# The second attention pass reads regrouped queries and keys: a hybrid encoder layer on one core

## The chip, the core and the metric

The kernel runs as one program on one core of a Trainium2 chip. The metric is the device time of one execution in microseconds (us), as the median of the runs taken. In the text PE is TensorE (the matrix engine, PEld its weight loads), DVE is VectorE, ACT is ScalarE, POOL is GpSimd and SP is SyncE, whose queue issues most of the DMAs.

## The reference

One encoder layer on 2048 tokens of width 1024, in float32. After an RMS norm, one projection yields the inputs of two mixers: a bidirectional gated linear attention (GLA, 4 heads) and a dilated attention of 8 heads of width 64. Their outputs go through `w_out`, and a mixture of 32 experts follows. The change is in the dilated attention:

```
DILATED_PATTERNS = ((128, 1), (512, 4), (2048, 16))
for window, dilation in DILATED_PATTERNS:
    # tokens i with the same i mod dilation form a sequence; in it, |i - j| <= 64
    o, lse = banded_attention(to_classes(q), to_classes(k), to_classes(v), 64)
w = softmax(stack(lses)); o = sum over patterns of w * o
```

Pattern 0 takes the tokens as they stand. Pattern 1 takes every 4th token (4 classes of 512), pattern 2 every 16th (16 classes of 128).

## The kernel before, in words

The program goes through the projections (in which a first attention pass finds each row's maximum and sum), then a stage that holds the second attention pass and the whole GLA, then `w_out` with the router, then the experts. The change is in the second of these stages, about 759 to 1197 us of the profiled execution.

Queries and keys of a head lie in SBUF with their 64 features in the partitions and the 2048 tokens along the row. They are kept as a high and a low part, so `aq` and `ak` (high) and `bq` and `bk` (low parts, with two extra rows that subtract the joint log-sum) give one score block by two matmuls that accumulate. `att_load` brings them for one head, into `pb0` or `pb1` by the head's parity.

The pass has 8 heads of 24 steps, 8 for each pattern (`att_steps`). A step takes two blocks. `att_scores` first adds the band's mask by a matmul with an identity (line 619, or line 622 twice, for blocks whose masks differ), then runs the two matmuls of each block (lines 625 and 626): the block's 128 keys are the stationary operand, 256 queries stream. ACT writes the exponentials to a buffer `pt` (lines 630 and 632). `att_values` multiplies them with the values (line 660), four steps later (`ATT_LAG`); there are five `pt` buffers (`PPB`). For patterns 1 and 2 the operands are strided views: every 4th or every 16th token of the row, for keys and for queries. A step of pattern 1 takes one block each of two classes that are two apart (4 blocks a class); in pattern 2 a step's mask has half the width, and two steps share one call of `att_values`.

Beside it run GLA's pieces (`all_gla`), emitted at 0.9 of a piece per attention step: a state scan on DVE (lines 785 and 788), the decays (lines 363 to 388), the preparation (lines 750 to 763) and the output (lines 802 to 858), for each of 4 GLA heads in turn, so that one GLA head takes two attention heads. Its gates are loaded into `sg` (line 826), of which there are two buffers.

Each engine runs its instructions in order. The order is made at build time by a planner that simulates the engines; only the expert stage's order is written by hand. Buffers of a pool are given out by the same planner: the value tiles and the raw rows of `w_out` share three buffers `vt`.

Of the kernel before, what the change touches and what calls it, by code (L numbers as in the profile page):

```python
# [25 lines left out]
P = 128  # L26
# [16 lines left out]
GLA_WAIT = 6  # L43
ATT_LAG = 4
LEAD = 3
# [12 lines left out]
NRAW, NSPL, CRAW = 8, 4, 6  # L58
PPB = 5
PSS, PSO, PSG = 4, 1, 2  # L60
# [30 lines left out]
def tile_trunk(ctx, tc, x, norm1_w, w_in, gfw, gfb, gbw, gbb, gnw, w_out, norm2_w, rgw, rgb, rew, reb,  # L91
# [77 lines left out]
    def block(p, b):  # L169

        if p == 2:
            return (lambda t: t[:, b::16]), (lambda t: duo(t, b)), am[:, 768:896], 0
        st, c, j, nj = (1, 0, b, 16) if p == 0 else (4, *divmod(b, 4), 4)
        k0 = min(max(P * j - 64, 0), P * nj - 256)
        v = (P * j - k0) // 64
        return (lambda t: t[:, c::st][:, P * j:P * j + P]), (lambda t: t[:, c::st][:, k0:k0 + 256]), \
            am[:, 256 * v:256 * v + 256], k0 * st // 16

    def joint_lse(half, pS, tiles):
# [366 lines left out]
    pb = [cw_.enter_context(tc.tile_pool(name=n, bufs=1, reuse_waits="tile")) for n in ("pb0", "pb1")]  # L546
    WO = []
    with ExitStack() as cb:
        vp = cb.enter_context(tc.tile_pool(name="vp", bufs=3, reuse_waits="tile"))
        pp = cb.enter_context(tc.tile_pool(name="pp", bufs=PPB, reuse_waits="tile"))  # L550
# [5 lines left out]

        BB = [[pb[e].tile([P, S], F32R, name=n) for n in ("bq", "bk")] for e in range(2)]
        for bq, bk in BB:
            for t, one in ((bq, 0.0), (bk, 1.0)):
                G.memset(f32(t)[0:64], 0.0)  # L560
                V.memset(f32(t)[0:2], one)

        def att_load(h):

            aq, ak = [pb[h % 2].tile([P, S], F32R, name=n) for n in ("aq", "ak")]
            bq, bk = BB[h % 2]
            load_twice(SY, f32(ak), khS[h])
            for t, src in ((aq, qS[h, 0:128]), (bk[64:128], klS[h]), (bq[64:128], qS[h, 64:128]), (bq[0:2], qS[h, 128:130])):
                SY.dma_start(f32(t), src)
            return aq, ak, bq, bk  # L570

# [12 lines left out]
        def wout_load(k):  # L584

            raw = vp.tile([P, D], F32, name="vt")
            SY.dma_start(raw, w_out[0, k * P:(k + 1) * P, :])
            t = pb[k // 4].tile([P, 2, D], F32R, name=("aq", "ak", "bq", "bk")[k % 4])
            A.copy(t[:, 0], raw)
            (G if k < 4 else V).tensor_tensor(t[:, 1], raw, f32(t[:, 0]), op=ALU.subtract)  # L590
            WO.append(t)

# [4 lines left out]
        def att_steps():  # L597

            for h in range(8):
                for b in range(8):  # L600
                    yield h, 0, (b, b + 8)
                for b in range(8):
                    yield h, 1, (b, b + 8)
                for c in (0, 4, 1, 5, 2, 6, 3, 7):
                    yield h, 2, (c, c + 8)

        def att_scores(h, p, blocks):
            if h not in ATT:
                ATT[h] = att_load(h)
            aq, ak, bq, bk = ATT[h]  # L610
            ps = psS.tile([P, 512], F32, name="psS")
# [5 lines left out]

            if p or blocks[0] not in (0, 7):
                ATT["last"] = T.matmul(sv[:, :, o:o + n], identb, mask(0, 2), start=True, stop=False, skip_group_check=True)
# [3 lines left out]
            for e, b in enumerate(blocks):  # L623
                ks, qs, _, _ = block(p, b)
                T.matmul(sv[:, e], ks(ak), qs(aq), start=False, stop=False, skip_group_check=True)  # L625
                T.matmul(sv[:, e], ks(bk), qs(bq), start=False, stop=True, skip_group_check=True)  # L626
            if p < 2:
# [7 lines left out]
        def att_values(h, p, blocks, pts):  # L635
# [21 lines left out]
            if p == 2:  # L657
                val = [(b // 8, b, (m, b % 8), pts[e // 2][:, 256 * (e % 2) + 64 * m:256 * (e % 2) + 64 * m + 64]) for m in range(2) for e, b in enumerate(blocks)]
            for hf, b, d, src in val:
# [12 lines left out]
        def attention():  # L672
            steps = list(att_steps())
            pend = []
            LAG = ATT_LAG
            for t in range(len(steps) + LAG):
                if t < len(steps):
                    h, p, blocks = steps[t]
# [12 lines left out]
                if t >= LAG:  # L691
                    h, p, blocks, pt = pend.pop(0)
                    if p < 2:
                        att_values(h, p, blocks, [pt])
                    elif t % 2 == LAG % 2:
                        ATT["even"] = blocks, pt
                    else:
                        b1, p1 = ATT.pop("even")
                        att_values(h, p, b1 + blocks, [p1, pt])
                    if (t - LAG) % 24 == 23:  # L700
# [92 lines left out]
        def gla_out(g):  # L793
# [30 lines left out]
            def gate_load(i4):  # L824
                sg = gs.tile([P, 4, P], F32, name="sg")
                SY.dma_start(sg, ggS[512 * i4:512 * i4 + 512, cols].rearrange("(i p) n -> p i n", p=P))
                return sg
# [49 lines left out]
        def all_gla():  # L877
# [6 lines left out]
            for g in range(4):  # L884
                yield from gla_scan(g)
                if g < 3:
# [5 lines left out]
        work2 = all_gla()  # L892
        lz = gp.tile([P, 192], F32, name="lz")
        work3 = joint_lse(1, psS, lambda n: gs.tile([P, 4, P], F32, name=(None, "oe", "sg", "sg")[n]).rearrange("p i n -> p (i n)")
                          if n else lz)
        cred = 0.0
# [799 lines left out]
```

## Time and profile before

| | us |
|---|---|
| median of 3 runs (2322.39 to 2325.31) | 2322.49 |
| the profiled execution | 2324.34 |
| its span from the first to the last instruction | 2322.6 |
| PE busy | 2112.9 (91%) |
| DVE busy | 1409.6 (61%) |
| ACT busy | 1281.8 (55%) |
| POOL busy | 1014.8 (44%) |

Busy time is a sum over stages that have different limits; an engine's share of the whole span says little about one stage. A matmul's record covers its latency, and successive matmuls overlap, so the cost of one to PE is the distance from its start to the next one's start.

### The profile page before, as it was taken

The page shows a single profiled execution, that of the slowest core. Times are in us where ns is not written, and L with a number is a line of the kernel's source. Part 1 is how long each engine was busy: PE and PEld are TensorE (multiplying, and loading weights), DVE is VectorE, ACT ScalarE, POOL GpSimd, SP SyncE. Part 2 cuts the span into 40 slices and gives each one's busy share as a digit, 9 for nine tenths or more (in the row PEclk, how much of TensorE's full clock was granted, in tenths as well). Part 3 has the DMA queues.
Part 4 walks back from the last instruction along what each step waited for, and adds up shares of the span by engine and source line. Part 5 has one row for each costly group of instructions (what it writes and reads, how often), then busy time and mean ns, then how long its engine had stood idle before and what let it go on. Part 6 is the DMA issues. An engine that isn't in the chain of part 4 may idle for free.

```text
span 2322.6 us, 38346 instructions
## 1 busy us (share of the span) xinstructions
PE 2112.9 (91%) x13813; PEld 1710.3 (74%) x13813; DVE 1409.6 (61%) x2871; ACT 1281.8 (55%) x2286; POOL 1014.8 (44%) x602
## 2 busy tenths in 40 slices
PE   7999998989799799999979999588898999999975
PEld 6888897989799677878768887366665666666654
DVE  7865544545365373626434666479876777768676
ACT  5222666657486464747442333356665767676744
POOL 4766111020120111202020001388887998888866
PEclk9999999999999899999989999799999999999988
DMA  8745765575642969685454643688988999999973
GB/s 308 233 107 151 183 181 163 149 207 147 175 124 69 217 152 187 145 193 113 114 149 151 212 155 127 214 269 282 328 272 279 327 326 329 300 317 295 310 279 151
DMA packets 283475, 487.09 MB, mean 210 GB/s; under 512 B 77079, under 2 KB 155927, under 8 KB 276096
## 3 DMA queue, kind: packets, MB, share of 16 engines
q1 hardware_dynamic: 238512, 368.40, 51.1%
q0 software_dynamic: 29344, 110.03, 17.0%
q10 hardware_dynamic: 15424, 6.16, 1.1%
q8 instruction: 110, 1.80, 0.3%
q14 instruction: 85, 0.70, 0.1%
HBM read 392.01 MB, written 94.44 MB: 209 GB/s over the span
## 4 chain that ended last, share of the span: by engine, by line
PE 71%; DVE 13%; DMA 9%; issue 3%; ACT 2%; POOL 1%; SPq 1%; ACTq 0%; another core or an unknown queue 0%; DVEq 0%; POOLq 0%
DMA wraw<-in_w_in_dram 5%; PE pg L1315 4%; PE pg L1317 4%; PE pg L1316 4%; DVE wlo L991 4%; PE psm L161 3%; PE po L1302 3%; PE psm L150 3%; PE psm L152 3%; PE psm L162 3%; PE psm L151 3%; PE psm L160 3%; PE po L1076 3%; PE po L1074 3%; PE po L1078 3%
## 5 line engine op out<-in xcount | busy, mean ns | idle before, releaser
L991 POOL TENSOR_TENSOR wlo<-raw,whi 128x2048 fp32r<-128x2048 f32 x97 | 513.3, 5302 | 87.0 <-ACT whi L986 83.0
L991 DVE TENSOR_TENSOR wlo<-raw,whi 128x2048 fp32r<-128x2048 f32 x95 | 372.6, 3931 | 64.0 <-ACT whi L986 64.0
L986 ACT CAST whi<-raw 128x2048 fp32r<-128x2048 f32 x192 | 366.8, 1910 | 53.2 <-PE pg L1383 36.6
L161 PE MATMUL psm<-wl,uhi 128*128 128x256 f32 (+1 forms) x768 | 222.9, 291 | 1.1 <-DVE wl L142 1.1
L160 PE MATMUL psm<-wh,uhi 128*128 128x256 f32 (+1 forms) x768 | 222.7, 290 | 0.7 <-ACT wh L141 0.5
L162 PE MATMUL psm<-wh,ulo 128*128 128x256 f32 (+1 forms) x768 | 221.6, 289 | 0.0
L1315 PE MATMUL pg<-whi,xh 128*128 128x512 f32 x512 | 215.7, 421 | 0.7 <-ACT xh L141 0.7
L495 ACT ACTIVATE je<-st,nm 128x256 bf16<-128x256 f32 (+1 forms) x384 | 178.6, 466 | 52.3 <-DVE nm L492 50.3
L1317 PE MATMUL pg<-wlo,xh 128*128 128x512 f32 x512 | 204.7, 400 | 0.0
L1316 PE MATMUL pg<-whi,xl 128*128 128x512 f32 x512 | 204.3, 399 | 0.0
L630 ACT ACTIVATE pt<-psS 128x512 f32<-128x512 f32 x128 | 131.0, 1074 | 85.3 <-PE psS L626 46.1
L625 PE MATMUL psS<-aq,ak 128*128 128x256 f32 x384 | 172.2, 455 | 0.0
L142 DVE TENSOR_TENSOR wl<-wraw,wh 128x512 fp32r<-128x512 f32 (+1 forms) x140 | 100.6, 738 | 92.5 <-ACT wh L141 92.1
L150 PE MATMUL psm<-uhi,wh 128*128 128x512 f32 (+1 forms) x400 | 153.8, 388 | 0.3 <-ACT wh L141 0.3
L151 PE MATMUL psm<-ulo,wh 128*128 128x512 f32 (+1 forms) x400 | 153.5, 385 | 0.5 <-DVE ulo L142 0.5
L152 PE MATMUL psm<-uhi,wl 128*128 128x512 f32 (+1 forms) x400 | 152.6, 385 | 0.0
L160 PEld LDWEIGHTS psm<-wh,uhi 128*128 128x128 f32 x768 | 150.5, 196 | 1.6 <-ACT wh L141 1.0
L161 PEld LDWEIGHTS psm<-wl,uhi 128*128 128x128 f32 x768 | 150.3, 196 | 1.6 <-DVE wl L142 1.3
L162 PEld LDWEIGHTS psm<-wh,ulo 128*128 128x128 f32 x768 | 149.1, 194 | 0.0
L492 DVE CUSTOM_DVE_ANT_0 st<-psS,am 128x256 f32<-128x256 f32 x256 | 98.6, 421 | 82.9 <-PE psS L483 57.5
L626 PE MATMUL psS<-bq,bk 128*128 128x256 f32 x384 | 141.5, 374 | 0.0
L141 ACT CAST wh<-wraw 128x512 fp32r<-128x512 f32 (+1 forms) x144 | 85.1, 623 | 97.3 <-DMA wraw<-in_w_in_dram 85.6
(420 smaller groups left out, 5097.1 us busy)
## 6 DMA issues: line engine op xcount, KB each, us to landing
raw<-in_expert_w_gate_dram SPq DMA_DIRECT2D x128, 512.0 KB
raw<-in_expert_w_up_dram SPq DMA_DIRECT2D x128, 512.0 KB
raw<-in_expert_w_down_dram SPq DMA_DIRECT2D x64, 1024.0 KB
wraw<-in_w_in_dram SPq DMA_DIRECT2D x128, 256.0 KB
xt<-in_x_dram SPq DMA_DIRECT2D x32, 512.0 KB
aq<-s_q POOLq DMA_DIRECT2D x8, 1024.0 KB, 8.3
kk<-s_khi POOLq DMA_DIRECT2D x16, 512.0 KB, 13.4
ak<-s_khi SPq DMA_DIRECT2D x16, 512.0 KB
```

The source lines that it names most:

```text
L150: T.matmul(ps[:m, ts], wh[:, k, m0:m0 + m], uh[:, k, ts], start=(k == 0), stop=False)
L151: T.matmul(ps[:m, ts], wh[:, k, m0:m0 + m], ul[:, k, ts], start=False, stop=False)
L152: T.matmul(ps[:m, ts], wl[:, k, m0:m0 + m], uh[:, k, ts], start=False, stop=(k == KD - 1))
L160: T.matmul(ps[:, :n], uh[:, k, sl], wh[:, k, :n], start=(k == 0), stop=False)
L161: T.matmul(ps[:, :n], uh[:, k, sl], wl[:, k, :n], start=False, stop=False)
L162: T.matmul(ps[:, :n], ul[:, k, sl], wh[:, k, :n], start=False, stop=(k == KD - 1))
L495: A.activation(je[:, :n], st[:, :n], AF.Exp, bias=nm[:, col:col + 1], scale=-1.0, accum_out=zt[:, col:col + 1])
L986: (A.copy if high is A else high.tensor_copy)(hi, raw)
L991: low.tensor_tensor(lo, raw, f32(hi), op=ALU.subtract)
L1315: T.matmul(pgt[n], xh[:, k], hi[:, 2 * n + kk], start=(k == 0), stop=False)
L1316: T.matmul(pgt[n], xl[:, k], hi[:, 2 * n + kk], start=False, stop=False)
L1317: T.matmul(pgt[n], xh[:, k], lo[:, 2 * n + kk], start=False, stop=(k == KD - 1))
```

## The change

Keys and queries of patterns 1 and 2 are first copied into contiguous tiles.

- Queries: `aq` and `bq` become one tile `qq` (both parts side by side). `in_order`, called at every second step from the 7th on, has POOL copy one group of 512 queries with both parts into a tile `grp` (two buffers): a whole class of pattern 1 in one instruction of 1024 elements a partition, or four classes of pattern 2 in two instructions of 512.
- Keys: `keys_in_order`, called one step ahead, has DVE copy the step's two key blocks, by one instruction of 256 elements for the high and one for the low part, into a tile `kgr` (two buffers).
- The steps' order: a step of pattern 1 takes two blocks of one class, and those at a class's ends need two masks. Pattern 2 goes through the classes in order, and each step has its own call of `att_values`.
- The values lag three steps, with four `pt` buffers; `vt` has two buffers and `sg` one.

```diff
-ATT_LAG = 4
+ATT_LAG = 3
-PPB = 5
+PPB = 4
+    def near(p, b):
+        j, nj = (b, 16) if p == 0 else (b % 4, 4)
+        k0 = min(max(P * j - 64, 0), P * nj - 256)
+        return slice(k0, k0 + 256)
-        vp = cb.enter_context(tc.tile_pool(name="vp", bufs=3, reuse_waits="tile"))
+        vp = cb.enter_context(tc.tile_pool(name="vp", bufs=2, reuse_waits="tile"))
+        def in_order(h, p, g):
+            qq = ATT[h][2]
+            ATT["grp", h, p, g] = t = vp.tile([P, 2, 512], F32R, name="grp", bufs=2)
+            if p == 1:
+                G.tensor_copy(t, qq.rearrange("p e (m c) -> p e c m", c=4)[:, :, g])
+            else:
+                for x in range(2):
+                    G.tensor_copy(t[:, :, 256 * x:256 * x + 256].rearrange("p e (y l) -> p e y l", y=2),
+                                  qq.rearrange("p e (l c) -> p e c l", c=16)[:, :, 8 * x + 2 * g:8 * x + 2 * g + 2])
+        def keys_in_order(h, p, blocks):
+            t = vp.tile([P, 2, 2, P], F32R, name="kgr", bufs=2)
+            for w in range(2):
+                src = ATT[h][w]
+                if p == 1:
+                    c, j = divmod(blocks[0], 4)
...
+                else:
+                    src = src.rearrange("p (l c) -> p c l", c=16)[:, blocks[0]::8]
+                V.tensor_copy(t[:, w], src)
+            ATT["keys", h, p, blocks] = t
-                for b in range(8):
-                    yield h, 1, (b, b + 8)
-                for c in (0, 4, 1, 5, 2, 6, 3, 7):
+                for c in range(4):
+                    yield h, 1, (4 * c + 1, 4 * c + 2)
+                    yield h, 1, (4 * c, 4 * c + 3)
+                for c in range(8):
                     yield h, 2, (c, c + 8)
-            if p or blocks[0] not in (0, 7):
+            if blocks[0] % 4 if p == 1 else p or blocks[0] not in (0, 7):
-                ks, qs, _, _ = block(p, b)
-                T.matmul(sv[:, e], ks(ak), qs(aq), start=False, stop=False, skip_group_check=True)
-                T.matmul(sv[:, e], ks(bk), qs(bq), start=False, stop=True, skip_group_check=True)
+                x = slice(256 * (b // 8), 256 * (b // 8) + 256) if p == 2 else near(p, b)
+                for w, kt in enumerate((ak, bk)):
+                    T.matmul(sv[:, e], kg[:, w, e] if p else kt[:, P * b:P * b + P], qq[:, w, x], start=False, stop=(w == 1), skip_group_check=True)
+                n = t % 24 - 6
+                if t < len(steps) and 0 <= n < 16 and n % 2 == 0:
+                    in_order(steps[t][0], 1 + n // 8, n // 2 % 4)
+                if t + 1 < len(steps) and steps[t + 1][1]:
+                    keys_in_order(*steps[t + 1])
-                    if p < 2:
-                        att_values(h, p, blocks, [pt])
-                    elif t % 2 == LAG % 2:
-                        ATT["even"] = blocks, pt
-                    else:
-                        b1, p1 = ATT.pop("even")
-                        att_values(h, p, b1 + blocks, [p1, pt])
+                    att_values(h, p, blocks, [pt])
-                sg = gs.tile([P, 4, P], F32, name="sg")
+                sg = gs.tile([P, 4, P], F32, name="sg", bufs=1)
```

The high parts of `w_out` that were loaded into `aq` and `bq` at the stage's end now go to the two halves of `qq`, and the small tiles of the joint log-sum share the `oe` and `sg` buffers.

## Rows read from the trace of the kernel before

**Rows 1.** Windows: the stage and its tail; busy us per engine, PE clock, DMA share, GB/s

```profile
759.00:1197.00 438.00, 407.19 (x4383) 339.19 (x4381) 208.19 (x459) 250.71 (x427) 69.85 (x63) 0.95 0.70 155
1197.00:1217.00 20.00, 4.21 (x58) 2.99 (x56) 6.55 (x20) 5.94 (x7) 0.43 (x2) 0.61 0.78 225
```

**Rows 2.** Timeline of PE: a step of pattern 0 (start, length, line, operands)

```profile
1101.10 0.39 PE L619 MATMUL psS<-am,identb 128*128 128x512 bf16 x1
...
1101.56 0.28 PE L625 MATMUL psS<-aq,ak 128*128 128x256 f32 x1
1101.68 0.28 PE L626 MATMUL psS<-bq,bk 128*128 128x256 f32 x1
1101.88 0.66 PE L660 MATMUL pso<-pt,vt 128*64 128x128 f32 x8
1102.47 0.39 PE L622 MATMUL psS<-am,identb 128*128 128x256 bf16 x2
...
1103.27 0.66 PE L660 MATMUL pso<-pt,vt 128*64 128x128 f32 x8
```

**Rows 3.** Timeline of PE: a step of pattern 1

```profile
1103.86 0.39 PE L619 MATMUL psS<-am,identb 128*128 128x512 bf16 x1
...
1104.52 0.44 PE L625 MATMUL psS<-aq,ak 128*128 128x256 f32 x1
1104.76 0.43 PE L626 MATMUL psS<-bq,bk 128*128 128x256 f32 x1
1105.12 0.66 PE L660 MATMUL pso<-pt,vt 128*64 128x128 f32 x8
```

**Rows 4.** Timeline of PE: a step of pattern 2

```profile
857.85 0.28 PE L619 MATMUL psS<-am,identb 128*128 128x256 bf16 x1
...
859.02 0.65 PE L660 MATMUL pso<-pt,vt 128*64 128x128 f32 x6
```

**Rows 5.** Windows: patterns 1 and 2 of heads 0 to 7, in order

```profile
770.50:818.80 48.30, 36.53 (x313) 29.93 (x311) 17.25 (x31) 15.81 (x22) 5.72 (x4) 0.86 1.04 199
835.30:876.70 41.40, 40.93 (x476) 33.60 (x475) 28.12 (x44) 31.93 (x57) 12.00 (x11) 1.00 0.56 122
888.20:926.30 38.10, 33.54 (x304) 28.07 (x303) 9.61 (x27) 14.98 (x22) 1.01 (x1) 0.91 0.83 158
943.80:983.20 39.40, 38.38 (x441) 31.98 (x441) 25.74 (x37) 31.54 (x63) 12.83 (x12) 1.00 0.49 115
1001.20:1035.30 34.10, 33.13 (x297) 27.22 (x295) 6.92 (x17) 13.65 (x21) 0.00 (x0) 1.00 0.76 154
1051.00:1092.10 41.10, 40.69 (x477) 33.37 (x475) 27.59 (x45) 30.09 (x53) 8.46 (x8) 1.00 0.35 73
1103.90:1141.80 37.90, 34.51 (x295) 28.36 (x294) 5.44 (x13) 16.81 (x29) 1.01 (x1) 0.91 0.55 126
1157.10:1200.00 42.90, 41.91 (x544) 35.85 (x544) 17.77 (x44) 23.90 (x58) 11.60 (x10) 1.00 0.37 106
```

**Rows 6.** One line's instructions: a strided DVE copy and a DVE instruction of one element

```profile
L203 DVE COPY sg<-oe x2: 260/263/266, 813.3 to 813.5; 64x128 f32<-64x128 f32 x2
...
L260 DVE TENSOR_SCALAR ss<-ss x16: 133/144/154, 7.0 to 134.5; 128x1 f32<-128x1 f32 x16
```

**Rows 7.** Groups of POOL by line and shape: count, busy us, mean ns

```profile
L590 POOL TENSOR_TENSOR aq<-vt,aq 128x1024 fp32r<-128x1024 f32 x1 | 2.4, 2382 | 46.6 <-ACT aq L589 46.6
...
L711 POOL TENSOR_SCALAR_AFFINE_SELECT tri<-tri 64x64 int8<-64x64 int8 x2 | 0.5, 236 | 2.2 <-DVE tri L708 2.2
masks.py:199 POOL TENSOR_SCALAR_AFFINE_SELECT ident<-ident 128x128 f32<-128x128 f32 x1 | 0.3, 294 | 0.1
```

**Rows 8.** Timeline of DVE around 2231 us, in the expert stage

```profile
2230.88 5.01 DVE L1557 TENSOR_SCALAR xl<-xg,tokl 128x1024 fp32r<-128x1024 f32 x1 [0.82 <-PE pg L1316]
2235.81 0.74 DVE L1557 TENSOR_SCALAR xh<-xg,tokl 128x1024 fp32r<-128x1024 f32 x1
```

**Rows 9.** Timeline of POOL at the same time

```profile
2230.76 4.59 POOL L991 TENSOR_TENSOR wlo<-raw,whi 128x2048 fp32r<-128x2048 f32 x1 [4.96 <-ACT whi L986]
```

More of the change, by code (lines that the diff above doesn't have):

```diff
@@ L546, in tile_trunk @@
     pb = [cw_.enter_context(tc.tile_pool(name=n, bufs=1, reuse_waits="tile")) for n in ("pb0", "pb1")]
-    WO = []
+    WO, WQ = [], {}
     with ExitStack() as cb:
-        vp = cb.enter_context(tc.tile_pool(name="vp", bufs=3, reuse_waits="tile"))
+        vp = cb.enter_context(tc.tile_pool(name="vp", bufs=2, reuse_waits="tile"))
         pp = cb.enter_context(tc.tile_pool(name="pp", bufs=PPB, reuse_waits="tile"))
@@ L555, in tile_trunk @@
         psG = cb.enter_context(tc.tile_pool(name="psG", bufs=PSG, space=PSUM, reuse_waits="tile"))
[L557 to L561, printed above, removed]
+        QQ = [pb[e].tile([P, 2, S], F32R, name="qq") for e in range(2)]
+        BK = [pb[e].tile([P, S], F32R, name="bk") for e in range(2)]
@@ L563, in att_load @@
+        for qq, bk in zip(QQ, BK):
+            G.memset(f32(qq)[0:64, 1], 0.0)
+            G.memset(f32(bk)[0:64], 0.0)
+            V.memset(f32(bk)[0:2], 1.0)
         def att_load(h):
-            aq, ak = [pb[h % 2].tile([P, S], F32R, name=n) for n in ("aq", "ak")]
-            bq, bk = BB[h % 2]
+            ak = pb[h % 2].tile([P, S], F32R, name="ak")
+            qq, bk = QQ[h % 2], BK[h % 2]
             load_twice(SY, f32(ak), khS[h])
-            for t, src in ((aq, qS[h, 0:128]), (bk[64:128], klS[h]), (bq[64:128], qS[h, 64:128]), (bq[0:2], qS[h, 128:130])):
+            for t, src in ((qq[:, 0], qS[h, 0:128]), (bk[64:128], klS[h]), (qq[64:128, 1], qS[h, 64:128]), (qq[0:2, 1], qS[h, 128:130])):
@@ L569, in att_load @@
                 SY.dma_start(f32(t), src)
-            return aq, ak, bq, bk
+            return ak, bk, qq
+        def in_order(h, p, g):
[7 more added lines that the diff above has]
+                                  qq.rearrange("p e (l c) -> p e c l", c=16)[:, :, 8 * x + 2 * g:8 * x + 2 * g + 2])
@@ new lines, in keys_in_order @@
+        def keys_in_order(h, p, blocks):
[4 more added lines that the diff above has]
+                    c, j = divmod(blocks[0], 4)
+                    src = src[:, c::4].rearrange("p (j m) -> p j m", j=4)[:, 0:4:3] if j == 0 else src[:, c::4].rearrange("p (j m) -> p j m", j=4)[:, 1:3]
+                else:
+                    src = src.rearrange("p (l c) -> p c l", c=16)[:, blocks[0]::8]
+                V.tensor_copy(t[:, w], src)
+            ATT["keys", h, p, blocks] = t
@@ L587, in wout_load @@
             SY.dma_start(raw, w_out[0, k * P:(k + 1) * P, :])
-            t = pb[k // 4].tile([P, 2, D], F32R, name=("aq", "ak", "bq", "bk")[k % 4])
+            if k % 4 < 2:
+                WQ[k] = pb[k // 4].tile([P, 2, S], F32R, name="qq") if k % 4 == 0 else WQ[k - 1]
+                t = WQ[k][:, k % 4].rearrange("p (a n) -> p a n", a=2)
+            else:
+                t = pb[k // 4].tile([P, 2, D], F32R, name=("ak", "bk")[k % 2])
             A.copy(t[:, 0], raw)
@@ L609, in att_scores @@
                 ATT[h] = att_load(h)
-            aq, ak, bq, bk = ATT[h]
+            ak, bk, qq = ATT[h]
+            if p:
+                qq = ATT["grp", h, p, blocks[0] // 4 if p == 1 else blocks[0] // 2]
+                kg = ATT.pop(("keys", h, p, blocks))
             ps = psS.tile([P, 512], F32, name="psS")
@@ L657, in att_values @@
             if p == 2:
-                val = [(b // 8, b, (m, b % 8), pts[e // 2][:, 256 * (e % 2) + 64 * m:256 * (e % 2) + 64 * m + 64]) for m in range(2) for e, b in enumerate(blocks)]
+                val = [(b // 8, b, (m, b % 8), pts[0][:, 256 * e + 64 * m:256 * e + 64 * m + 64]) for m in range(2) for e, b in enumerate(blocks)]
             for hf, b, d, src in val:
@@ L892, in tile_trunk @@
         work2 = all_gla()
-        lz = gp.tile([P, 192], F32, name="lz")
-        work3 = joint_lse(1, psS, lambda n: gs.tile([P, 4, P], F32, name=(None, "oe", "sg", "sg")[n]).rearrange("p i n -> p (i n)")
-                          if n else lz)
+        work3 = joint_lse(1, psS, lambda n: gs.tile([P, 4, P], F32, name=("oe", "oe", "sg", "oe")[n], bufs=1 if n == 2 else 2).rearrange("p i n -> p (i n)"))
         cred = 0.0
```

## The prediction

> **What bounds the kernel now.** I read the windows first, then the timeline of PE inside them. In the stage of the second attention pass PE is busy for 407 of 438 us, DVE for 208, ACT for 251 and POOL for 70 [rows 1]: PE is the limit and the other engines look half idle. The timeline shows what PE's time buys. A step of pattern 0 takes 0.78 us from its mask to the next work (1101.10 to 1101.88), and its score matmuls start 0.12 us apart [rows 2]. A step of pattern 1 takes 1.26 us (1103.86 to 1105.12), with starts 0.24 us apart [rows 3], and one of pattern 2 takes 1.17 us (857.85 to 859.02), though its mask is half as wide [rows 4]. The matmuls have the same size in all three; what differs is that the operands are strided. The reader is to see that PE is busy at half speed in two thirds of the steps. Last come the windows by head: where patterns 1 and 2 run, DVE has two faces, 26 to 28 of some 40 us in heads 1, 3 and 5 (GLA's decays and output run there), but 5 to 17 of 34 to 48 in the even heads [rows 5].
>
> **Gain on PE.** With contiguous operands a middle step of pattern 1 should cost what pattern 0's does: 1.26 - 0.78 = 0.48 us saved, 32 steps, 15.4 us. A step at a class's ends now pays two half masks; pattern 0 has such steps too, at 0.80 us (1102.47 to 1103.27) [rows 2], so 0.46 x 32 = 14.7 us. In pattern 2 the mask is 0.28 us long instead of 0.39 [rows 2, 4], so a step should cost 0.78 - 0.11 = 0.67: 0.50 x 64 = 32.0 us. Sum 62 us, 7.75 a head. The value matmuls stay the same in number and size. That all of it is on the path holds as long as nothing else becomes late; ACT's 251 us [rows 1] fit into what is left.
>
> **Key copies on DVE.** Two per step in 128 steps, 256 in all, 32 a head, of 256 elements with a strided source. The nearest row is a strided copy of 128 elements: 0.263 us; an instruction of one element takes 0.144 [rows 6]. So an element costs (0.263 - 0.144) / 128 = 0.93 ns, and a copy 0.144 + 0.238 = 0.38 us. Bounds: 0.26 if the length is nearly free, 0.53 if everything scales. I take 0.38: 12.2 us a head, 97 in all. On average there is room (208 + 97 = 305 of some 400 us). By stretch there isn't. Heads 1, 3 and 5 need 28.1 + 12.2 = 40.3 of 41.4 us, 37.9 of 39.4 and 39.8 of 41.1 [rows 5], so even with DVE never idle they can shrink by only 1.1, 1.5 and 1.3 us instead of 7.75 each: 19 us of the 62 are gone, and 43 are left. Head 7 needs 30.0 of 42.9 and the even heads at most 29.5 of 48.3; these keep theirs.
>
> **Query copies on POOL.** Eight groups a head, 64 in all, each of 1024 elements a partition. No row shows a copy on POOL. Below, two one-input instructions of 64 and 128 elements took 0.236 and 0.294 us, 0.9 ns an element, so 1.1 us a group; above, a two-input one of 1024 elements took 2.38 us [rows 7]. A copy has one input, so I take 1.35 us, nearer the lower end, with something for the stride and for pattern 2's second instruction. That is 86 us in all; POOL itself has the room (70 of 438 busy). The price is elsewhere: DVE's 1024-element instruction on one tensor took 5.01 us where its twin took 0.74, and it ended at 2235.89, just after POOL's instruction that had begun 0.12 us before it and ended at 2235.35 [rows 8, 9]. DVE instructions of this kind stand still while POOL has an operand in hand, and a key copy is of this kind. Where DVE is the limit (heads 1, 3 and 5: 24 groups) I count half a group's 1.35 us, since GLA's instructions that read PSUM fill the rest: 24 x 0.67 = 16 us. In the other heads two steps take 2 x (1.85 - 0.49) = 2.7 us (1.85 from mask 1103.86 to the next step's by the same pattern: 1.26 for scores [rows 3] and 0.59 for the values, as from 1101.88 to 1102.47 [rows 2]), and a group with four key copies wants 1.35 + 1.52 = 2.9: covered to 0.2 us, counted as nothing. If that cover is gone, rival 2 has the price.
>
> [...]
>
> **Given back.** GLA's work on DVE that the copies push aside in heads 1, 3 and 5 can slide into the even heads, where DVE is idle for most of the time [rows 5]. The planner decides; I count a quarter of the 19 + 16 us, 9. Ends: nothing, and all of it.
>
> **Edits at nothing or little.** One buffer less with a lag one shorter leaves the same spare `pt` buffer: nothing, where ACT keeps up as now. One `sg` buffer makes SP hold the next gate load, and every load queued behind it, until the last gate is used; the gate is due a pass later, and only where the DMA share is near 1 (heads 0, 2 and 4 [rows 5]) is it late: 2 us. Two `vt` buffers delay the last `w_out` rows, but PE is busy for 4.2 of the 20 us after the stage [rows 1]: nothing, up to 5 if they come more than that late. In head 0 PE is idle for 11.8 of 48.3 us with the DMAs saturated (share 1.04) [rows 5]; a key copy that the planner put behind a GLA instruction waiting for its load makes that longer: 3 us, between 0 and 8. In general DVE's queue is now on PE's path, since the two `kgr` buffers allow one step's lead.
>
> **Sum.** 62 - 19 - 16 + 9 - 5 = 31 us. The profiled execution took 2324.34 us (1.7 more than its span), 1.85 above the median; 2324.3 - 31 = 2293.3, on the median's scale 2291.5, so 2292.
>
> **Rivals.**
> 1. PE's gain comes nearly whole: the planner spreads GLA, so that DVE's full stretches level out, and POOL's copies are near 1.1 us. For it: 305 us of DVE in some 390. Against it: heads 1, 3 and 5 as they stand. 62 less some 7: 2267.
> 2. Slower: the copies take turns. A group holds DVE's key copies for 1.5 us or more of a time near 2.4 us, with keys only one step ahead. Then patterns 1 and 2 need DVE's time plus 8 x 1.5 = 12 us a head: heads 1, 3 and 5 take 52.3, 49.9 and 51.8 us, 32 more than now; head 7 takes 42.0, 0.9 less; heads 0, 2, 4 and 6 take 41.5, 33.8, 31.1 and the PE floor of 30.2, which saves 6.8, 4.3, 3.0 and 7.7. Sum 32 - 23 = +9, and 5 to 9 for the small terms and a clock that falls in the gaps (0.86 and 0.91 in the stretches where PE waits now [rows 5]): 2322.5 + 16 = 2338. It decides from about 1.3 us blocked a group. For it: rows 8 and 9; against it: POOL's one-input rows. [...]
> 3. The lock and DVE's queue eat just what PE gains: 1.2 us a group gives -6 by the same sum, with 5 of small terms 2321.
>
> That contiguous operands don't run faster is no rival: pattern 0 on the same lines shows it.
>
> **Chances and range.** Forecast (10 to 45 us gained) 0.55; rival 1 0.12; rival 2 0.20; rival 3 0.13. A measurement tells 0.2%, 4.6 us, from no change. Of rival 3 0.08 stay within that, 0.05 are faster: faster 0.55 + 0.12 + 0.05 = 0.72, same 0.08, slower 0.20. The range reaches to most of rival 1 and half of rival 2: 2267 to 2337. The forecast's own is 2278 to 2312.
>
> **What would show it.** Starts of lines 625 and 626 should be 0.12 us apart in all patterns; if they stay at 0.24, the first term falls. Key copies should last 0.38 us alone and up to a group longer where a POOL copy stands beside them; if none is longer, the lock is no matter, and rival 1 gains. PE should wait for `kgr` in heads 1, 3 and 5 above all, hardly in the even ones. POOL copies over 2 us, with PE waiting for DVE in every pair of steps, would make me wrong on the far side.

## Result and profile after

The changed kernel took 2393.13 us (median of 4 runs, 2383.95 to 2404.39) against 2322.59 of the kernel before on the same chip (4 runs): 1.0299 times as long, 95% interval 1.0266 to 1.0332. Forecast were 2292 us and a range of 2267 to 2337. The profiled execution of after took 2404.39 us, 80.1 more than that of before, and it is the slowest of the four; ratios come from all runs, places and durations from this one execution.

Where its 80.1 us lie (first and last score matmul, and first matmul of `w_out`, bound the stretches):

| stretch | before | after | change |
|---|---|---|---|
| start to first score | 759.0 | 779.1 | +20.1 |
| stage, first to last score | 437.8 | 482.4 | +44.6 |
| handover, last score to first `w_out` matmul | 20.3 | 32.0 | +11.7 |
| the rest of the span | 1105.5 | 1109.2 | +3.7 |

Of the first line some 12 us are there at the last projection matmul, and most of them arise between 233 and 268 us, in code that the change doesn't touch and with the DMAs full (share 1.18 from 230 to 250 us, 1.15 in before). The kernel without copies was profiled twice: at 268 us it stood 2.2 us behind the kernel before in one execution and 7.7 in the other. So up to some 8 us of the 20 are variation from run to run. In the rest PE waits for `identb` on DVE just before the first score, 13.9 us against 5.7 before.

The windows of after, the stage and the handover (columns as in [rows 1], which they answer):

```profile
779.10:1261.50 482.40, 410.93 (x4447) 318.45 (x4445) 374.91 (x708) 247.84 (x424) 209.14 (x155) 0.91 0.59 133
1261.50:1293.50 32.00, 3.20 (x27) 2.08 (x26) 7.91 (x24) 8.61 (x11) 5.69 (x5) 0.55 0.70 202
```

DVE is busy for 375 us instead of 208, where 305 were expected; POOL for 209 instead of 70. PE's time outside its busy 411 us rises from 31 to 71, its busy time doesn't fall (407 before), and its mean granted clock falls from 0.95 to 0.91. The part of the change that concerns PE works, though. Its timeline shows a middle and an end step of pattern 1 (start, length, line, operands), against [rows 2, 3]:

```profile
858.03 0.39 PE L658 MATMUL psS<-am,identb 128*128 128x512 bf16 x1
858.07 0.82 PE L665 MATMUL psS<-grp,kgr 128*128 128x256 f32 x4
858.82 0.66 PE L699 MATMUL pso<-pt,vt 128*64 128x128 f32 x8
859.41 0.39 PE L661 MATMUL psS<-am,identb 128*128 128x256 bf16 x2
859.56 0.72 PE L665 MATMUL psS<-grp,kgr 128*128 128x256 f32 x4
860.21 0.33 PE L699 MATMUL pso<-pt,vt 128*64 128x128 f32 x2
```

From mask to values it takes 0.79 us (858.03 to 858.82) where it took 1.26. What went wrong is in the copies. The groups of DVE and of POOL in the stage (count, busy us, mean ns, idle time before them and its end):

```profile
L600 DVE CAST kgr<-bk 128x256 fp32r<-128x256 f32 x126 | 89.3, 709 | 0.1
L600 DVE CAST kgr<-ak 128x256 fp32r<-128x256 f32 x126 | 79.3, 630 | 34.3 <-PE psS L665 33.4
...
L388 DVE TENSOR_TENSOR_SCAN tab<-rm,tab 64x512 f32<-64x512 bf16 x24 | 38.6, 1608 | 6.9 <-POOL tab L385 6.7
```

```profile
L587 POOL CAST grp<-qq 128x512 fp32r<-128x512 f32 x64 | 73.9, 1184 | 62.7 <-PE psS L665 62.7
L584 POOL CAST grp<-qq 128x1024 fp32r<-128x1024 f32 x30 | 67.5, 2251 | 118.0 <-PE psS L665 105.3 <-issue 12.6
```

A key copy takes 0.63 or 0.71 us in the mean. Its median is 0.38 (the one line's instructions: shortest, median, longest ns, and who waited for them):

```profile
L600 DVE CAST kgr<-ak x128: 360/391/2286, 764.4 to 1259.0; 128x256 fp32r<-128x256 f32 x128
L600 DVE CAST kgr<-bk x128: 358/383/5937, 766.2 to 1259.3; 128x256 fp32r<-128x256 f32 x128
...
  PE psS L665: 27.1, 17
  PEld psS L665: 17.6, 12
```

The mean is made by copies that stand beside one of POOL's. One such moment, in DVE's timeline and in POOL's:

```profile
925.50 0.38 DVE L600 CAST kgr<-ak 128x256 fp32r<-128x256 f32 x1
925.80 2.22 DVE L600 CAST kgr<-bk 128x256 fp32r<-128x256 f32 x1
927.93 0.37 DVE L600 CAST kgr<-ak 128x256 fp32r<-128x256 f32 x1
```

```profile
925.68 2.09 POOL L584 CAST grp<-qq 128x1024 fp32r<-128x1024 f32 x1 [3.79 <-PE psS L665]
```

POOL begins at 925.68 and ends at 927.77; the key copy that begins 0.12 us later ends at 928.02, and the next one is short again. It is what [rows 8, 9] showed for another pair of instructions. Nor is it one moment only: of all 256 key copies 64 took over 0.7 us, each of them beside an instruction of POOL (59 beside a query copy); of the 115 that overlap none of POOL's, none took over 0.41 us.

### The profile page after: what moved, and what is told of

The parts are those of the page before. It is cut to its first block, busy times and chain, and to the rows that moved or that the text cites. A ratio compares the mean times of both kernels' runs of the same rounds, so it can differ in the third digit from the quotient of the medians.

```text
span 2402.7 us, 38970 instructions
## 1 busy us (share of the span) xinstructions
PE 2118.0 (88%) x13845; PEld 1690.2 (70%) x13845; DVE 1593.7 (66%) x3125; ACT 1280.4 (53%) x2286; POOL 1161.7 (48%) x698
## 4 chain that ended last, share of the span: by engine, by line
PE 65%; DVE 17%; DMA 9%; issue 4%; ACT 3%; POOL 1%; SPq 0%; ACTq 0%; DVEq 0%; another core or an unknown queue 0%; POOLq 0%
DMA wraw<-in_w_in_dram 5%; PE pg L1352 4%; PE pg L1353 4%; PE pg L1354 4%; DVE wlo L1028 4%; PE psm L161 3%; PE psm L162 3%; PE psm L160 3%; PE psm L150 3%; PE psm L151 3%; PE psm L152 3%; PE po L1339 3%; DVE kgr L600 3%; PE po L1111 3%; PE po L1113 3%
## 5 line engine op out<-in xcount | busy, mean ns | idle before, releaser
L1028 DVE TENSOR_TENSOR wlo<-raw,whi 128x2048 fp32r<-128x2048 f32 x95 | 385.5, 4066 | 64.6 <-ACT whi L1023 64.6
L699 PE MATMUL pso<-pt,vt 128*64 128x128 f32 (+3 forms) x1856 | 143.9, 267 | 12.5 <-ACT pt L669 7.3
L665 PE MATMUL psS<-grp,kgr 128*128 128x256 f32 x512 | 113.7, 335 | 27.4 <-DVE kgr L600 27.1
```

The source lines that it names most:

```text
L1028: low.tensor_tensor(lo, raw, f32(hi), op=ALU.subtract)
```

## The experiments

The runs come from several chips, on which the kernel before took 2322 to 2327 us. So kernels are compared by their ratio to the kernel before on the same chip, and a difference of ratios is given in us of 2323; the medians only stand beside them. Theory 1: POOL's copies hold DVE, and PE waits for DVE. Theory 2: the keys are copied only one step ahead. Theory 3: the side edits cost the time. The table has the 18 runs; "waits" is the stage less PE's busy time in it, the engines' columns are busy us in the stage. Places and durations come from one profiled execution of each kernel.

| kernel | median us | ratio, 95% interval | stage | waits | DVE | ACT | POOL | handover |
|---|---|---|---|---|---|---|---|---|
| before | 2322.59 | 1 | 437.8 | 30.8 | 208 | 251 | 70 | 20.3 |
| after | 2393.13 | 1.0266-1.0332 | 482.4 | 71.5 | 375 | 248 | 209 | 32.0 |
| e1 no copies | 2317.02 | 0.9948-1.0002 | 438.8 | 25.7 | 208 | 251 | 62 | 9.9 |
| e16 the same again | 2321.86 | 0.9964-1.0009 | 435.9 | 24.1 | 207 | 251 | 62 | 10.1 |
| e2 queries, POOL | 2373.00 | 1.0177-1.0230 | 463.4 | 39.1 | 227 | 252 | 200 | 32.5 |
| e3 keys, DVE | 2369.60 | 1.0147-1.0217 | 461.4 | 24.2 | 298 | 252 | 66 | 31.2 |
| e4 queries ACT, keys DVE | 2347.66 | 1.0062-1.0143 | 441.5 | 46.2 | 290 | 356 | 66 | 33.7 |
| e5 queries, ACT | 2353.62 | 1.0063-1.0160 | 441.6 | 31.3 | 206 | 357 | 59 | 33.5 |
| e6 short POOL copies | 2410.61 | 1.0346-1.0432 | 507.0 | 76.5 | 326 | 245 | 303 | 31.2 |
| e7 as e4, keys 3 ahead | 2347.65 | 1.0052-1.0121 | 443.6 | 62.4 | 284 | 357 | 67 | 32.6 |
| e8 as after, keys 3 ahead | 2393.06 | 1.0261-1.0347 | 478.5 | 88.2 | 359 | 246 | 212 | 35.4 |
| e9 queries ACT and DVE | 2333.60 | 1.0017-1.0066 | 424.9 | 59.2 | 323 | 303 | 69 | 33.8 |
| e10 as e9, four row buffers | 2332.71 | 1.0010-1.0067 | 422.9 | 57.6 | 323 | 303 | 69 | 30.1 |
| e11 as e10, even heads | 2347.14 | 1.0050-1.0112 | 441.7 | 44.4 | 262 | 276 | 64 | 28.7 |
| e12 as after, even heads | 2362.83 | 1.0102-1.0202 | 449.2 | 43.4 | 277 | 249 | 133 | 33.5 |
| e13 as e10, rows earlier | 2327.00 | 0.9997-1.0040 | 424.1 | 55.8 | 323 | 302 | 69 | 28.9 |
| e14 as e13, half copies | 2337.13 | 1.0031-1.0078 | 432.9 | 61.6 | 329 | 307 | 70 | 29.5 |
| e15 as e14, GLA rate 1.0 | 2344.41 | 1.0060-1.0117 | 445.0 | 70.6 | 328 | 310 | 70 | 27.2 |
| e17 as e9, keys 1 ahead, own pool | 2340.46 | 1.0050-1.0100 | 443.5 | 40.7 | 327 | 300 | 72 | 17.0 |
| e18 as after, own pool | 2378.08 | 1.0192-1.0258 | 483.6 | 68.0 | 378 | 247 | 212 | 14.3 |

**No copies, one copy, and ACT in POOL's place.** e1 drops both calls and reads the old strided views, e2 keeps the query copies, e3 the key copies, e4 moves the query copies:

```
e1, e2 -  if t + 1 < len(steps) and steps[t + 1][1]: keys_in_order(*steps[t + 1])
e1, e3 -  if t < len(steps) and 0 <= n < 16 and n % 2 == 0: in_order(...)
e4     -  G.tensor_copy(t, qq.rearrange(...)[:, :, g])     # and pattern 2's
       +  A.copy(t, qq.rearrange(...)[:, :, g])
```

> The changed kernel without its query copies on GpSimd and its key copies on DVE: the scores read the strided operands as before, and every other edit stays (order of the steps, values lag 3, four pt, two vt, one sg buffer, the query tile of two rows). Theory 1 (GpSimd's copies hold back DVE's key copies and the other DVE instructions, and PE waits for these): the loss is gone with the copies, 2325 to 2345 us, with score starts 0.24 us apart again; what is above 2322.5 is the price of the side edits. Theory 2 (DVE's queue is too full and only one step ahead, GpSimd or not): the same here. Theory 3 (the side edits cost the time, above all at the stage's two ends): 2375 us or more, since PE also loses its 62 us again.

> The kernel without any copies once more, for its interval: the side edits alone (one order of the steps, lag 3, other buffers). From the first time, 0.9975 of the kernel before; expected 0.994 to 1.000, 2312 to 2325 us. If the 10 us come from the handover (9.9 us from the last score to the first w_out matmul against 20.3), they show again.

2317 and, repeated, 2322 us (0.998 and 0.999 of before): with every side edit in place nothing is lost, so theory 3 falls as it was stated, and e1 lies under the range of theory 1, which had a price for these edits. It is not shown to be faster either. The 10 us of handover did show again.

> The changed kernel with the query copies on GpSimd alone; the keys are read strided, and DVE copies nothing. Theory 1: GpSimd's copies still hold back DVE, but only GLA's instructions, on which PE does not wait step by step. If the moving operand's stride is what doubles the matmul, PE keeps most of its 62 us: 2280 to 2315 us, score starts 0.12 us apart, no PE wait for DVE in pairs of steps. If the stationary operand's stride is what costs, starts stay at 0.24 us and the time is 2325 to 2350. Theory 2: as theory 1, DVE has no key copies here. Theory 3: 2360 or more.

> The changed kernel with the key copies on DVE alone; the queries are read strided, and GpSimd copies nothing. Theory 1: without GpSimd's copies a key copy lasts 0.38 us throughout (mean under 0.45 against 0.63 and 0.71 us), and PE does not wait for them for more than some 5 us in all; the time is that of no copies within 10 us if the moving operand sets the matmul's length, 30 to 50 us less if the stationary one does. Theory 2 (DVE's queue alone is the trouble): PE waits for the key tile in heads 1, 3 and 5 as it does with both copies (over 20 us), and the time is 2365 us or more.

e2 lies above both ranges of theory 1. e3 lies in the branch of theory 2: 2370 us, with 20 us of waits for the keys. Four score matmuls of an end step in e2's PE timeline, with the next line's start:

```profile
916.63 0.47 PE L664 MATMUL psS<-grp,ak 128*128 128x256 f32 x1
916.93 0.40 PE L664 MATMUL psS<-grp,bk 128*128 128x256 f32 x1
917.17 0.40 PE L664 MATMUL psS<-grp,ak 128*128 128x256 f32 x1
917.40 0.40 PE L664 MATMUL psS<-grp,bk 128*128 128x256 f32 x1
917.73 0.72 PE L698 MATMUL pso<-pt,vt 128*64 128x96 f32 x12
```

and in e3's:

```profile
905.79 1.18 PE L664 MATMUL psS<-qq,kgr 128*128 128x256 f32 x4
906.89 0.44 PE L698 MATMUL pso<-pt,vt 128*64 128x128 f32 x4
```

Four take 1.10 us with either operand strided (916.63 to 917.73, 905.79 to 906.89), with starts 0.23 to 0.30 us apart in e2 and 0.24 with both strided in [rows 3], and 0.65 to 0.75 with neither (859.56 to 860.21, 858.07 to 858.82). One copy alone buys almost nothing on PE, and neither was free: e2's stage is 25 us longer than e1's, e3's 23. In e3 the mean key copy was 0.42 us, as theory 1 had it, but PE still waited 20 us for the keys, 10.5 of them at once in head 0. Yet e3's waits in all are no longer than e1's (24.2 and 25.7): its 23 us show up as busy time of PE, which the part on e4 takes up.

> Both copies as in the changed kernel, but the query copies are issued by ACT instead of GpSimd (96 instructions of 512 or 1024 elements; an estimate of 0.6 to 1.3 us each, 80 us on an engine that is busy for 251 of 438). Theory 1: key copies return to 0.38 us (mean under 0.45), DVE's busy time in the stage falls from 375 to about 305 us, and the time to 2310 to 2340 us, unless ACT's exponentials become late in their turn. Theory 2: key copies are short but PE still waits for the key tile over 20 us, 2360 us or more. Theory 3: 2370 or more.

The key copies in e4's stage, with the number of after's:

```profile
L600 DVE CAST kgr<-ak 128x256 fp32r<-128x256 f32 x126 | 53.0, 420 | 40.6 <-PE psS L665 39.5
L600 DVE CAST kgr<-bk 128x256 fp32r<-128x256 f32 x126 | 48.2, 382 | 0.1
```

With the same 708 instructions DVE's busy time falls from 375 to 290 us, and the ratio from 1.030 to 1.010: some 46 us. Of PE's waits in the stage DVE ended 52 us in after, 21 in e4 and 7 before. So theory 1 is shown as far as POOL's copies hold DVE and PE waits for it. The 46 us are the price of POOL as a whole: the same edit also takes the copies out of GLA's way in POOL's queue, and the two aren't separated. But 2348 is above the 2310 to 2340 us expected and no gain against before: the stage is as long as without copies, the handover 13 us longer than before, and ACT has the copies now:

```profile
L587 ACT CAST grp<-qq 128x512 fp32r<-128x512 f32 x64 | 65.4, 1081 | 0.0
L584 ACT CAST grp<-qq 128x1024 fp32r<-128x1024 f32 x30 | 61.2, 2040 | 0.0
```

A strided group of pattern 1 takes 2.04 us on ACT, nearly as long as on POOL (2.25); the 0.6 to 1.3 us an instruction stated before the run were an estimate. What PE's time went into, from each PE start to the next, summed by line over the stage:

```
                     before   e1    after   e4    e10
scores               213.5  221.1  170.6  156.9  164.6
masks                 10.7   14.5   48.2   43.9   31.7
values               120.9  108.3  146.3  137.4  125.6
GLA's matmuls         92.5   94.7  116.9  103.3  100.9
```

The scores gained 43 to 57 us against before, near the 62 forecast (which include the shorter masks). The others gave it back: masks, behind which the scores stand waiting for keys, values waiting for exponentials, and GLA.

Not all of this is waiting. With the same matmuls PE is busy in the stage for 366 us in e9, 395 in e4, 403 in e17 and 411 in after. Two things in the traces lengthen its busy time. Where the planner's order alternates scores and values, a score comes every 0.63 us with two value matmuls between (after, 1196.49 to 1197.12), while four scores in a row take 0.75 us and eight value matmuls 0.59 (858.82 to 859.41), both at a granted clock of 1.00:

```profile
1196.49 0.39 PE L665 MATMUL psS<-grp,kgr 128*128 128x256 f32 x1
1196.81 0.38 PE L699 MATMUL pso<-pt,vt 128*64 128x96 f32 x2
1197.12 0.39 PE L665 MATMUL psS<-grp,kgr 128*128 128x256 f32 x1
```

PE changes from one kind of matmul to another 818 times in e3's stage and 817 in e17's, against 737 in e1's and 720 in e9's. The second thing is the clock. The granted clock was 0.50 instead of 1.00 for 90 us of after's stage, 40 of before's and 44 of e9's. In one such stretch (columns as in [rows 1], granted clock 0.50) contiguous scores, here of pattern 0, start 0.21 us apart:

```profile
904.00:916.00 12.00, 8.44 (x41) 6.45 (x41) 9.78 (x16) 4.70 (x8) 8.30 (x6) 0.50 1.10 228
```

```profile
912.94 0.41 PE L665 MATMUL psS<-qq,bk 128*128 128x256 f32 x1
913.15 0.41 PE L665 MATMUL psS<-qq,ak 128*128 128x256 f32 x1
913.36 0.41 PE L665 MATMUL psS<-qq,bk 128*128 128x256 f32 x1
```

Over after's stage the starts of neighbouring scores lie 0.214 us apart in the median at a granted clock of 0.50 and 0.119 at 1.00; the strided ones of pattern 1 in before lie 0.236 us apart at 0.50 and 0.238 at 1.00. So at 0.50 the copies save PE little. How the longer busy time divides between order and clock is open.

**Queries alone by ACT** (e2 with e4's edit):

> Query copies alone, by ACT; keys strided, nothing copied on GpSimd or DVE. The same with GpSimd's copies took 2373 us, no copies 2317; in both the score starts stay 0.23 us apart or so, hence PE gains little. Theory 1 (GpSimd's copies hold DVE, which here has only GLA's work, and stand before GLA's own steps in GpSimd's queue): with ACT these go, DVE's scans return to 1.22 us, 2325 to 2345 us. Rival (any 130 us of copies, or the order that the planner makes with them, cost the same): 2360 us or more.

2354, between the two. With no key copies on DVE at all, POOL's copies cost some 21 us more than ACT's (ratios 1.020 and 1.011), all of it in the stage (463.4 against 441.6); but ACT's aren't free.

**Shorter holds.**

```
-  G.tensor_copy(t, qq.rearrange(...)[:, :, g])
+  for x in range(8): G.tensor_copy(t[:, e, y], qq.rearrange(...)[:, e, g, y])    # 128 elements each
```

> The changed kernel with the same query copies on GpSimd, cut into instructions of 128 elements (8 a group instead of 1 or 2). Theory 1a (a GpSimd copy holds DVE for as long as the instruction runs, and what matters is the length of one hold): key copies of over 1 us nearly vanish, their mean falls from 0.69 us to under 0.5, and the time falls by 20 to 40 us, to 2355 to 2375. Theory 1b (what matters is GpSimd's whole time, of which DVE loses its share however it is cut, and GLA's instructions behind the copies in GpSimd's queue): 8 starts a group instead of 1 or 2 make GpSimd's time longer, key copies keep a mean over 0.6 us, and the time is 2385 us or more.

Key copies fell to a mean of 0.53 us, DVE's busy time to 326: shorter holds do let DVE in. But POOL's groups in e6's stage show what it cost:

```profile
L591 POOL CAST grp<-qq 128x128 fp32r<-128x128 f32 x256 | 121.0, 519 | 60.0 <-PE psS L669 59.8
L586 POOL CAST grp<-qq 128x128 fp32r<-128x128 f32 x244 | 119.0, 535 | 84.0 <-PE psS L669 77.9 <-issue 4.6 <-POOL grp L591 1.6
```

0.52 us a piece, 4.2 a group, POOL busy for 303 of 507 us; the ratio rose from after's 1.030 to 1.039, some 21 us. Each theory had half of it, and the run doesn't separate them further.

**Keys three steps ahead** (the head's output tile shares the group buffers for room):

```
-  t = vp.tile([P, 2, 2, P], F32R, name="kgr", bufs=2)      + bufs=4
-  if t + 1 < len(steps) ...: keys_in_order(*steps[t + 1])  + t + 3
```

> Query copies by ACT as in the kernel before this one of that kind, and the key copies are issued three steps ahead into four buffers instead of one step ahead into two (the head's output tile takes a buffer of the query groups, to make room). Theory 2 (one step ahead is too little): PE's waits at the mask and the first score matmul for the key tile go, some 26 us in the mask's rows and 16 in the waits named; the time falls from 2348 to 2315 to 2330 us. Theory 4 (ACT with 356 of 441 us and its 2 us copies in front of the exponentials is the limit): PE waits for ACT's tiles instead, the time stays at 2340 to 2355.

> The changed kernel, query copies on GpSimd, with key copies three steps ahead in four buffers. Theory 1 (DVE's time itself is stretched by GpSimd's copies, 375 of 482 us busy, over 40 of each head's p1 and p2 in heads 1, 3 and 5): a longer lead covers single holds of 2 us but not the sum, the key copies stay at a mean over 0.6 us; 2355 to 2380 us, heads 1, 3 and 5 change least. Theory 2 (the short lead alone made it slower): PE's waits for the key tile go, 2330 us or less.

No change in either: 1.009 after e4's 1.010, and 1.030 as in after. In e7 PE's wait for keys fell to one of 5.7 us, and waits for ACT and for GLA's tiles took its place (theory 4). In e8 key copies stayed at 0.63 us; that it would still gain 13 us or more was wrong. PE waited for the key tile no more, but DVE still ended 56 us of its waits (52 in after), now at GLA's tiles. So the time that DVE loses comes out at its other work when the keys get a lead. As the main cause theory 2 falls.

**ACT and DVE share the queries** (no POOL, keys three ahead):

```
+  A.copy(dst[:, 0], src[:, 0])
+  V.tensor_copy(dst[:, 1], src[:, 1])
```

> No GpSimd copies: of each query group ACT copies the first 512 elements a partition (about 1.0 us by the rows of the kernel with ACT copies) and DVE the other 512 (an estimate of 0.5 to 0.65 us, from 0.38 for 256); keys three steps ahead. By these ACT has some 252 + 65 = 317 us and DVE 208 + 97 + 38 = 343 of the stage. Theory 2 and 4 together (with room on both engines PE's 66 us show up): a stage of 390 to 415 us and 2285 to 2310 us in all, faster than before by 0.5 to 1.5 per cent. If instead the GLA chain's latency sets the stage (its DVE and ACT steps late behind copies, whichever engine makes them), the stage stays at 435 or more, 2335 us or more.

The stage is 424.9, 13 us shorter than before and 19 shorter than e7's: the first kernel to gain there, but short of the 390 to 415 us expected. It still lost 0.4% in all, by a handover of 33.8 us. PE's waits in e9's stage (total us, times, longest), none of them the main one; the one for `identb` ends with the stage's first mask:

```profile
PE pso L700 <- ACT pt L672: 9.5, 6, 3.1
PE psS L662 <- DVE identb L631: 9.4, 1, 9.4
PE psg L821 <- DVE ss L828: 8.7, 14, 1.3
PE psS L666 <- DVE kgr L601: 6.7, 1, 6.7
PE psS L666 <- DVE grp L589: 6.6, 3, 6.2
```

**Even heads only** (the calls and the new operands under `h % 2 == 0`):

> The changed kernel (query copies on GpSimd, key copies on DVE one step ahead) with copies in heads 0, 2, 4 and 6 only. If the loss comes from GpSimd holding DVE in the GLA heads alone (as the prediction had it), the even heads keep their 7.75 us each: 2295 to 2315 us. If GpSimd's copies cost wherever they stand (DVE held for 2.2 us a group, keys late), the even heads gain nothing or lose: 2335 to 2365 us.

> As the kernel before it in this list, with copies in heads 0, 2, 4 and 6 only; heads 1, 3, 5 and 7 read strided operands. In the kernel with copies in all heads, patterns 1 and 2 of the even heads were 4 to 12 us shorter than with none and those of the odd heads at best 3. If the odd heads gain nothing because DVE and ACT are full of GLA's steps there, leaving them out costs nothing and gives the engines back: stage 400 to 420 us, 2295 to 2315 us in all. If it is the sum over the stage that counts, half the copies give half the gain: stage 425 to 435, 2320 to 2332.

e12: from each head's first mask of pattern 1 to the next head's first mask, patterns 1 and 2 of heads 0, 2, 4 and 6 took 156 us with POOL's copies and 158 in e1, where 31 were to be gained, and the odd heads' pattern 0 behind them grew from 15 to 21 us in the mean. So the copies cost wherever they stand, not in heads 1, 3 and 5 alone. e11 missed on the slow side: by the same stretches its even heads gained 17 us, but pattern 0 of the odd heads grew to 20 us in the mean. Why half the copies gave less than half is open.

**The handover.** e10 adds two group buffers for the last `w_out` rows, e13 loads them earlier, e14 and e15 try the stage on top:

```
e10 -  raw = vp.tile([P, D], F32, name="vt")     + name="vt" if k < 4 or k % 2 else "grp"
e13 +  ... or t > 7 * 24 + 20 and 4 <= len(WO) < 8: wout_load(len(WO))
e17, e18 +  kq = ...tile_pool(name="kq", bufs=2, ...)    # behind the other pools; grp and kgr in it
```

> As the kernel in which ACT and DVE share the query copies, with the last rows of w_out loaded in turn into value buffers and query-group buffers (four instead of two). If the wait for these buffers in SP's queue is what delays the first loads of the mixing stage (issued 19.3 us after the last score there, 7.5 before), these start 8 to 12 us sooner, PE's first matmul of w_out comes 20 to 26 us after the last score instead of 33.8, and the time falls by as much, to 2320 to 2326 us. If other waits are behind it, the time stays at 2330 to 2337.

> As the kernel with the last w_out rows in value and query-group buffers, with these rows loaded during the last three steps and not after them. If the handover is the rows' place in SP's queue, the first mixing loads are issued within 8 us of the last score and the first w_out matmul comes 18 to 24 us after it (30.1 before this edit): 2320 to 2326 us, no change against the kernel before within its interval. If the handover stays near 30, something else holds these loads, and the time is 2330 or more.

> As the kernel before it in this list, with every query group copied in two halves one step apart: ACT 256 elements at a time (an estimate of 0.55 us from 1.05 for 512), DVE the same (about 0.38). If copies in front of exponentials and key copies are what PE waits for (8 us for the query groups by ACT, 7 by DVE, 12 for exponentials), some 10 to 15 of these go: 2308 to 2318 us. If it is GLA's chain, nothing changes within 4 us.

> As the kernel before it in this list, with GLA's steps interleaved at a rate of 1.0 instead of 0.9 to a step of attention. Attention's steps are shorter now, so that GLA's chain may be what ends late: then the stage falls by 5 to 10 us. If DVE is the limit, GLA's steps only move, and the time stays within 5 us or rises.

3.7 us of handover with e10 and 1.2 more with e13, less than forecast. e13 is the best with copies: 2327.0, the same as before within its interval. e14 made the stage 9 us longer, which neither branch of its expectation had; e15 made it 12 longer still, the branch in which GLA's steps only move. Smaller pieces and another rate of GLA are no cure.

> The changed kernel (query copies on GpSimd) with the group and key tiles in a pool of their own, nothing else. If the place makes the handover long: 32 us become 10 to 15, and the time falls from 2393 to 2370 to 2378. The stage, where GpSimd's copies hold DVE, stays at 470 to 490. If it isn't the place: 2385 us or more.

> Query copies shared by ACT and DVE, key copies one step ahead as in the changed kernel, and the group and key tiles in a pool of their own behind the other pools, so that the value tiles lie as in the kernel without copies. If the place of the new tiles in SBUF makes the handover long, it falls from 29 to 34 us to 10 to 15, with the stage still at 423 to 432: 2303 to 2315 us, faster than the kernel before by 0.3 to 0.9 per cent. If it isn't the place, the handover stays near 30 and the time at 2325 to 2340.

This was it. SP's timeline of after at the handover:

```profile
1270.59 9.29 SPq L618 DMA_DIRECT2D vt<-in_w_out_dram  x4
1279.97 0.38 SPq L1092 DMA_DIRECT2D gl<-s_gla  x1
```

and of e18, whose last score is at 1254.3:

```profile
1260.92 0.83 SPq L1093 DMA_DIRECT2D gl<-s_gla  x2
1263.66 4.35 SPq L619 DMA_DIRECT2D vt<-in_w_out_dram  x2
```

In after the first loads of the mixing stage stand behind all four `w_out` rows, 18.5 us after the last score; in e18 they go ahead of the last rows, 6.6 us after. The handover is 14.3 instead of 32.0, the ratio 1.0225 instead of 1.030, some 17 us. All that e18 changes is where the new tiles lie; with them in the pool of the value tiles, the planner made the other order. That the place acts through this order is read from the two timelines and not tested by itself; moving the rows alone (e13) gave 1.2 us. e17's handover fell as well (17.0), but its stage was 443.5 again, which neither branch of its expectation had. PE waited 19.9 us for keys there (10.6 at once in head 0), yet its waits in all fell from e9's 59.2 to 40.7; what grew is its busy time, from 366 to 403. Whether the shorter lead or the own pool made this order is open, as e17 changes both, and the output tile's buffer too. e13's stage and e18's handover together weren't run.

## Why the prediction was wrong

Its first terms held: a middle step at a granted clock of 1.00 takes 0.79 us for 0.78 forecast, the scores gave 43 to 57 us of the 62, and a key copy takes 0.38 us when it stands alone.

**The step that failed is "Query copies on POOL".** It had two sizes. A group was taken as 1.35 us, "nearer the lower end"; it took 2.25 us in pattern 1 and 2 x 1.18 in pattern 2. The nearest row by length, the two-input instruction of 1024 elements at 2.38 us in [rows 7], was the better measure than 64 and 128 elements of another operation; ACT's 2.04 us for the same strided group (e4) says that such a length isn't special to GpSimd.

Then the hold was counted for half a group in 24 groups, 16 us, and in the other heads as "covered to 0.2 us". Measured: the 252 key copies of the stage take 169 us instead of 96 (at 0.38), 73 more, or 1.1 to 1.2 us for each of the 64 groups. That is half of every group, not only of the 24 in heads 1, 3 and 5, and e12 shows it to cost in the other heads too. One sign held: of PE's 27.1 us of waits for the key tile 21.6 lie in heads 1, 3 and 5. That such instructions "stand still while POOL has an operand in hand" held for the copies that begin second: of after's key copies beside one query copy of 1024 elements alone, 23 of the 25 that begin during it end 0.23 to 0.27 us behind it, while the 17 that begin before it take 0.37 to 0.42 us. What makes them wait the traces don't show. "GLA's instructions that read PSUM" weren't held: lines 824 and 827 of after took 0.340 and 0.354 us in the mean, beside POOL's instructions as alone; line 879, which reads SBUF, took 0.91 instead of 0.34. By e4, which burdens ACT in its place, the choice of POOL costs some 46 us of the 70.

**"All of it is on the path as long as nothing else becomes late" failed as well.** Even without POOL much of the scores' gain turned into waits: 25 us of waits without copies, 56 to 62 with them on ACT and DVE (e7, e9, e13), though DVE and ACT were busy for no more than 284 and 357 of 444 us (e7) or 323 and 303 of 425 (e9). Sums of busy time as in "on average there is room" say little here: each step of PE needs a key tile from DVE (two copies), one exponential from ACT and every other step a group, in queues that also hold GLA's steps. Best case 15 us of stage (e10), not the 36 that 62 - 19 - 16 + 9 left. "Given back", 9 us, didn't show. Nor had the sum a term for the clock, which stood at 0.50 for 90 us of the stage.

**"Edits at nothing or little"** missed the handover: 0 up to 5 us were counted, 11.7 came, and not for the two `vt` buffers (e1 has them, and a handover of 9.9 us) but for the place of the tiles (e18). The start of the stage wasn't in the sum: besides run-to-run variation PE waits 8 us longer there for `identb` on DVE than before.

**The rivals.** Rival 2 had the right mechanism and sign, and was wrong by 55 us. From each head's first mask of pattern 1 to the next head's first mask, which is how the windows of [rows 5] run, its odd heads (52.3, 49.9 and 51.8) were measured at 44.2, 52.1 and 51.5, head 7 (42.0) at 32.8, and its even heads (41.5, 33.8, 31.1 and 30.2) at 40.9, 42.6, 40.4 and 36.4. So it missed in heads 2, 4 and 6, where it let DVE's time or PE's floor stand for the whole. By these stretches patterns 1 and 2 grew by 22 us; another 23 lie in the stretches of pattern 0 (119 to 142 us), into which the planner had put late steps of the head before and for which rival 2 had no term. Its "clock that falls in the gaps" was real, 0.95 to 0.91 in the stage and 0.88 in e6; what that clock costs the kernel as a whole no run tells, but a score matmul pays 0.214 us for 0.119.

## What to carry to other kernels

Before giving a copy to an idle engine, ask which engine it stops: here 141 us on an idle POOL cost DVE 73 us in the key copies alone, and what PE waited for DVE rose from 7 to 52 us. A gain of 0.5 us a step on the limiting engine is only worth the slack of the engines that must now deliver every step, in their queues' order and not in their busy sums. When only buffers were added, look at the ends of the stage: the place of tiles was worth some 17 us far from the edit, and with it the planner's order of loads changed.

## What the runs showed of the hardware

- One strided operand, moving or stationary, slowed the score matmuls of pattern 1 as much as two: four took 1.10 us with one (e2, e3) and 0.65 to 0.75 with neither (after); with both the starts lie 0.24 us apart [rows 3]. The elements read stand 4 apart there, and no run has a smaller step but that of contiguous elements.
- Copies of strided elements to fp32r cost 2.04 us for 1024 elements on ACT (e4; 1.04 for a contiguous row of `w_out`, e1) and 2.0 us at the least on POOL, 2.12 to 2.25 in the mean (e2, after); DVE took 0.65 us for 512 (e9).
- On POOL a copy of 128 elements took 0.52 us in the mean, so that eight make nearly twice the time of one of 1024 (e6, after).
- Contiguous score matmuls gain little at the lower clock: 0.119 us from start to start at a granted clock of 1.00 and 0.214 at 0.50, against 0.236 to 0.238 for the strided ones of pattern 1 at either level (after, before).
